# Split weight sums kept in device memory by the first FFN pass, and two variances taken together at a seam

## The chip, the cores and the metric

The kernel runs on one core of one Trainium2 chip. The metric is the device time of one execution in microseconds. A core has TensorE (matrix products into eight banks of PSUM), VectorE and ScalarE (elementwise work; both read PSUM), GpSimd (elementwise work on SBUF alone), and queues from which SyncE, ScalarE and GpSimd issue DMAs. Each engine runs its own instructions in the order in which they stand in its queue, and waits for other engines by semaphores.

## What is computed

One block of a transformer trunk in float32, 2048 tokens wide 1024. The first part (a spatial-gating mixer beside a memory attention, with its output projection and layer norm) is untouched by the change. The second part is this:

```
h = x @ w_in                                   # [2048, 1024] @ [1024, 5632]
y = (silu(h[:, :2816]) * h[:, 2816:]) @ w_down # [2048, 2816] @ [2816, 1024]
x = layer_norm(alpha * x + y) * g + b          # over the 1024 features
```

## The kernel before

Everything is feature-major: partitions hold features, columns hold tokens. TensorE takes float32 in the reduced form float32r, so each operand is **split** (`split`, line 71): ScalarE copies the value into a float32r tile (`hi`, line 73), VectorE subtracts that from the value (`lo`, line 74), and a product takes three matmuls, hi x hi, hi x lo and lo x hi (`PASSES`, line 95).

The FFN part runs in three passes over ranges of tokens (688, 680 and 680; here called pass one, two and three, `no` 0, 1 and 2 in the code). In a pass the width of 2816 is 22 tiles, in five blocks of 5, 4, 4, 4 and 5 (`FBLOCKS`). For each block, `up` makes the gated hidden tiles and `down` adds their part of the output into an accumulator of the pass (`acc`, tiles `fa`).

The up projection of one tile (one of gate and one of value, line 345) uses Strassen's scheme in Winograd's form: the weights of both tiles and both halves of the contraction form a 2 x 2 matrix, the tokens another, and seven products replace eight. Each product is 4 contraction tiles x 3 matmuls of 340 columns (344 in pass one). Its left operands are the weights themselves (a11, a12, a22, products 1, 2, 4) or sums of them (products 5, 6, 7, 3). `halves` (line 97) loads two tiles of 512 KB on SyncE's queue and makes the four sums:

```
engine.tensor_add(s1, a21, a22)        # line 109
engine.tensor_sub(s2, s1, a11)         # line 110
engine.tensor_sub(s3, a11, a21)        # line 112
lambda: engine.tensor_sub(s4, a12, s2) # line 113, called as the products begin
```

`engine` is GpSimd for the first block of each pass and VectorE for the others (line 347). `products` (line 115) then takes the products in the order 1, 6, 2, 5, 7, 3, 4: for each, a buffer `w` of the tag `wsp` (five buffers in all, shared with the weights of `down`), a split into it, twelve matmuls, and the stage behind it (lines 366 to 368), which reads PSUM. Products 1 and 2 share one bank: ScalarE copies it between them (line 366, `m1`); products 5 and 3, and 7 and 4, share banks in the same way, with VectorE's additions between them.

The right operands of a pass (`Pass.load`, line 319) are made while the last block of the pass before is projected down; GpSimd makes one of their sums (line 330). The layer norm of a pass is taken in small steps during the first block of the next pass: `norm_steps` (line 257) is a generator, and behind each product's stage one step is taken (line 373). So there are 5 x 7 = 35 places. GpSimd adds the features into `s_b` (lines 174, 176); `centre` takes the mean from TensorE, subtracts it on VectorE, squares on ScalarE, and adds the squares on GpSimd (line 197); `var` (line 220) brings the variances through TensorE to VectorE, which runs twelve small instructions (lines 227 and 280 to 285) and a diagonal tile `dg` (line 230); `spread` (line 234) has TensorE spread the result over the partitions; `finish` multiplies on VectorE, scales on ScalarE, and stores two feature tiles at a time on SyncE's queue (line 419). A pass has two such norms, one for each half of its tokens. What stays of the steps behind the first block's last product is run at once, and then `residual` loads the accumulator's start (line 383).

The framework orders each engine's instructions ahead of time from the program's order and its own estimate of when each can run; only TensorE's order is fixed as written (`in_order`, line 51).

Of the kernel before, what the change touches and what calls it, by code (L numbers as in the profile page):

```python
# [11 lines left out]
F32 = mybir.dt.float32  # L12
# [14 lines left out]
KD = D // P            # 8 contraction tiles of the model width  # L27
KB = (MIX + HEADS * HD) // P   # 10 contraction tiles of the branch width
NF = DFF // P          # 22 tiles of the FFN width
TC = 512               # tokens in a chunk of the mixer part  # L30
OPERANDS = (25, 3)             # operand tiles of the up projection that find room before and behind the mixer's end
NCHUNK = SEQ // TC
FPASSES = (688, 680, 680)      # tokens in a pass of the FFN part
# [6 lines left out]
def trunk_kernel(ctx, tc, xT, memT, wv, wuq, ws, bs, vg, vb, wmk, wmv, wo,  # L40
# [10 lines left out]
    def in_order(ins):  # L51
        """TensorE runs its instructions in the order in which they are emitted."""
        if last_on_pe:
            tc.add_manual_dep(ins.ins, last_on_pe.pop().name,
                              mybir.DependencyInfo(mybir.DependencyClass.NoSync, mybir.DependencyReason.DATA),
                              reason="order of TensorE")
        last_on_pe.append(ins.ins)
# [13 lines left out]
    def split(hi, lo, src, engine=nc.vector):  # L71
        """src = hi + lo exactly, each with the bits that one pass of TensorE carries."""
        nc.scalar.copy(hi, src)  # L73
        engine.tensor_sub(lo, src, hi.bitcast(F32))  # L74
# [4 lines left out]
    def weights(src, shape, name, loads=1):  # L79
        """src [P, *shape], loaded at once and split; as shape[0] pairs [P, 2, shape[1]], several to a tile."""  # L80
        k, r, pairs = shape[0], raw([P, *shape], f"r_{name}"), []
        for i in range(loads):
            s = slice(i * k // loads, (i + 1) * k // loads)
            nc.sync.dma_start(out=r[:, s], in_=src[:, s])
        parts = -(-k * shape[1] // 512)
        for i in range(parts):
            s = slice(i * k // parts, (i + 1) * k // parts)
            n = s.stop - s.start
            w = wsp([P, 2, n, shape[1]], f"w_{name}_{i}")
            split(w[:, 0], w[:, 1], r[:, s])  # L90
            pairs += [w[:, :, j, :] for j in range(n)]
        return pairs
# [4 lines left out]
    def halves(wa, wb, name, engine, in_place):  # L97
        """Two output tiles' weights, loaded: the left operands of the seven products in Strassen's scheme (in
        Winograd's form), over the two tiles x the halves of the contraction; by product."""
# [15 lines left out]
    def products(left, right, banks, name, stages, order, s4_after):  # L115
        """The seven products, into four banks; `stages` has the sums behind each of them."""
# [4 lines left out]
        for n, p in enumerate(order):  # L121
            if n == s4_after:
                s4()
            to, start, stop = out[p]
            w = wsp([P, 2, 4, P], f"w{p}_{name}")
            split(w[:, 0], w[:, 1], src[p])
            for k in range(4):
                for i, (a, b) in enumerate(PASSES):
                    matmul(to, w[:, a, k, :], right(p, k, b), start=start and k == 0 and i == 0,
                           stop=stop and k == 3 and i == 2, skip_group_check=True)  # L130
            stages[p]()

# [11 lines left out]
    def two_tiles(t, m, t0, n):  # L144
        """Feature tiles m and m + 1 of the tokens t0 to t0 + n."""
        return t[m * P:(m + 2) * P, t0:t0 + n].rearrange("(a p) t -> p a t", p=P)
# [4 lines left out]
    class Norm:  # L151
        """Takes y feature tile by feature tile. Its sums over the tiles run on GpSimd; or, to end soon, on TensorE
        behind a VectorE that takes two tiles at a time (`pairs`)."""
# [24 lines left out]
        def variances(self, sq, start, stop):  # L178
            """One accumulation group for all columns: its start opens the whole bank."""
# [77 lines left out]
    def norm_steps(norms, stores, wait, pad):  # L257
        """The norms in small steps, to be taken between other work."""
# [10 lines left out]
        for _ in range(pad):  # L269
            yield  # L270
        for x, store in zip(norms, stores):
            x.var()
            for _ in range(5):
                yield
            yield from pairs(lambda a, b: x.finish(store, a, b))

    def inv_sqrt(r, v, t):
        """r = v ** -0.5 on VectorE: Newton steps from an estimate made of the bits, half the exponent; t is scratch."""
# [8 lines left out]
    # ================= the mixer part =================  # L287
    open_pools = {}

    def pool(name, bufs, side="left"):  # L290
        """Pools lie one above the other, from either side of the memory."""
# [14 lines left out]
    class Pass:  # L306
        """A range of tokens through the FFN. Its up projection takes Strassen's scheme in Winograd's form, over
        [gate, value] tiles x halves of the model width x halves of the tokens: seven products for eight."""
# [10 lines left out]
        def load(self, k, keep=0):  # L319
            """The seven right operands, for contraction tiles k and k + 4; the last `keep` are left to rest()."""  # L320
# [24 lines left out]
        def up(self, f, work):  # L345
            no, h = self.no, self.h
            sums = nc.gpsimd if f < FBLOCKS[0] else nc.vector    # VectorE has the norm of the pass before at first
# [22 lines left out]
            def then(stage):  # L370
                def run():
# [3 lines left out]

            products(halves(w1[f], w1[NF + f], f"u{name}", sums, False), lambda p, k, b: self.x[p][k][:, b], banks,
                     name, {p: then(stage) for p, stage in stages.items()}, (1, 6, 2, 5, 7, 3, 4), 0)
# [9 lines left out]
        def down(self, blk, gs, f0, cut, done):  # L387
            """The block's part of the FFN's output, for the groups of token ranges of `cut` in turn."""
# [33 lines left out]
    # ================= the mixer part =================  # L422
# [21 lines left out]
    class Chunk:  # L444
        """512 tokens; the methods are emitted in the order in which TensorE is to run them."""
# [15 lines left out]
        def load(self, j):  # L461
            """Feature tiles j and j + 4 of the input."""
# [26 lines left out]
        def v_half(self, hooks):  # L489
            """The v half of the gate, token-major, and its norm."""  # L490
# [38 lines left out]
        def feature_major(self, a, t, name, act):  # L529
            """Output tiles a and a + 1 of the input projection, into t [P, 2, TC]; `act` is run on each part of it."""  # L530
# [19 lines left out]
        def scores(self, b):  # L550
            """Memory attention of 128 tokens: scores and softmax, token-major; heads in the order 0, 2, 1, 3."""
# [23 lines left out]
        def turn(self, b):  # L575
            """The softmax of 128 tokens with the memory on the partitions."""
# [28 lines left out]
        def mixed(self, j):  # L605
            """The v half, mixed over its 128 positions, feature-major."""
# [12 lines left out]
        def u_half(self, j):  # L619
            """The u half, feature-major."""  # L620
# [11 lines left out]
        def project(self, first, after):  # L632
            """Output projection and residual, of feature tiles j and j + 4 in turn."""
# [76 lines left out]
    def make_room(j, m):  # L710
        """Behind output tiles of the last chunk: room for the FFN, and its first operands."""
# [83 lines left out]
    # ================= the FFN part =================  # L795
# [9 lines left out]
    for no in range(len(FPASSES)):  # L805
# [3 lines left out]
        for blk, nb in enumerate(FBLOCKS):  # L809
# [7 lines left out]
            elif no < len(FPASSES) - 1:  # L817
# [10 lines left out]
                work = norm_steps(norms, [pa.store(0, h), pa.store(h, n)], 4, 0)  # L828
# [81 lines left out]
```

## Time and profile before

| what | value |
|---|---|
| timed runs | 2202.6 us median of 3 (2201.05 to 2203.41) |
| profiled execution, span | 2205.3 us, 34595 instructions |
| mean granted TensorE clock | 0.989 of full speed |
| first part, up to the first product of the FFN | 0 to 752 us |
| first block's up projection, pass one / two / three | begins at 752.1 / 1227.0 / 1707.7 us |
| moved by DMA | 221.93 MB, 101 GB/s on the mean |

The span is that of one execution taken by the profiler, which was not one of the timed runs; its span lies 2.7 us above their median. A page of the profile gives busy times of the engines; the trace behind it can be asked for busy times in a stretch of the span, for the waits of one engine (who waited, for which line of which engine, us in all, how often, the longest), for the instructions on one tile (duration least/median/most), and for the instructions in order of time. Lines are those of the kernel before. A matmul's own duration overlaps its neighbours', so the time of one matmul is taken from a stretch divided by the count in it.

### The profile page before, as it was taken

What the parts mean: (1) busy time and instruction counts of PE and PEld (TensorE: products, weight loads), DVE (VectorE), ACT (ScalarE), POOL (GpSimd) and SP (SyncE); (2) the same over time, 40 slices, a digit from 0 to 9 for tenths busy, and PEclk for the clock granted to TensorE, in tenths of its full rate; (3) what the DMA queues carried; (4) which work ended last, traced back from release to release, by engine and by line L of the source; (5) the groups of instructions that cost most, each with busy time, mean ns of one, the idle gap of its engine ahead of it and who ended that gap; (6) DMA issues with size and microseconds to landing.
All of it is one profiled execution on the core that took longest, in us unless ns stands there. A gap on an engine that the chain in (4) does not pass through costs nothing.

```text
span 2205.3 us, 34595 instructions
## 1 busy us (share of the span) xinstructions
PE 2120.0 (96%) x13130; PEld 2009.0 (91%) x13130; DVE 1704.4 (77%) x3014; ACT 970.7 (44%) x1886; POOL 397.3 (18%) x294
## 2 busy tenths in 40 slices
PE   9899999999999999999999889999999899999996
PEld 7888798798788889999999889999998899999996
DVE  7986796797788785776778986676689877677677
ACT  5553653654465452433434453343344534334344
POOL 1412321331322440000001820000004700000003
PEclk9999999999999999999999999999999999999998
DMA  6233324234334443212223242222224242221223
GB/s 211 77 110 123 112 78 158 92 96 149 117 96 133 139 132 92 87 58 86 87 68 91 89 160 88 82 68 82 82 66 119 83 153 67 87 86 58 89 75 99
DMA packets 88965, 221.93 MB, mean 101 GB/s; under 512 B 8416, under 2 KB 18656, under 8 KB 88800
## 3 DMA queue, kind: packets, MB, share of 16 engines
q1 hardware_dynamic: 88320, 218.66, 31.9%
q8 instruction: 103, 1.69, 0.3%
q0 software_dynamic: 480, 1.07, 0.2%
q14 instruction: 62, 0.51, 0.1%
HBM read 202.92 MB, written 16.78 MB: 100 GB/s over the span
## 4 chain that ended last, share of the span: by engine, by line
PE 66%; DVE 19%; DMA 5%; issue 4%; ACT 4%; POOL 2%; ACTq 0%; DVEq 0%; POOLq 0%; SPq 0%
PE h L60 36%; PE d L60 19%; PE v L60 5%; PE u L60 3%; DMA r_x<-in_xT 2%; DVE w L74 2%; DVE x L74 2%; DVE w_o L74 1%; DMA r_f<-x1d 1%; DVE w_u L74 1%; PE y L60 1%; POOL s_a L197 1%; ACT p L569 1%; DVE z L526 1%; DVE w_d L74 1%
## 5 line engine op out<-in xcount | busy, mean ns | idle before, releaser
L60 PE MATMUL h<-x,w 128*128 128x340 f32 (+1 forms) x5544 | 886.5, 322 | 14.7 <-DVE w L74 6.5
L60 PEld LDWEIGHTS h<-x,w 128*128 128x128 f32 x5544 | 875.1, 190 | 22.3 <-DVE w L74 8.9
L60 PE MATMUL d<-g,w_d 128*128 128x340 f32 (+3 forms) x3168 | 504.4, 320 | 7.5 <-DVE w_d L74 6.6
L60 PEld LDWEIGHTS d<-g,w_d 128*128 128x128 f32 x3168 | 497.4, 189 | 11.6 <-DVE w_d L74 8.3
L73 ACT CAST w<-s_u 128x512 fp32r<-128x512 f32 x264 | 163.4, 620 | 227.2 <-PE d L60 106.5
L74 DVE TENSOR_TENSOR w<-s_u,w 128x512 fp32r<-128x512 f32 x264 | 195.2, 741 | 46.1 <-ACT w L73 39.1
L60 PE MATMUL y<-br,w_o 128*128 128x512 f32 x960 | 224.4, 395 | 0.0
L60 PEld LDWEIGHTS y<-br,w_o 128*128 128x128 f32 x960 | 180.5, 188 | 42.0
L73 ACT CAST w<-r_u 128x512 fp32r<-128x512 f32 x198 | 122.3, 618 | 166.6 <-PE h L60 67.7
L60 PE MATMUL v<-w_v,x 128*128 128x512 f32 x768 | 188.4, 402 | 6.7 <-ACT w_v L73 5.0
L74 DVE TENSOR_TENSOR w<-r_u,w 128x512 fp32r<-128x512 f32 x198 | 150.0, 759 | 53.0 <-ACT w L73 49.7
L73 ACT CAST w_d<-r_d 128x512 fp32r<-128x512 f32 (+2 forms) x184 | 95.7, 521 | 206.6 <-PE d L60 151.3
L60 PEld LDWEIGHTS v<-w_v,x 128*128 128x128 f32 x768 | 144.1, 191 | 42.1 <-ACT w_v L73 5.0
L409 DVE TENSOR_TENSOR fa<-fa,d 128x340 f32<-128x340 f32 (+3 forms) x192 | 97.2, 506 | 100.3 <-PE d L60 100.3
L330 POOL TENSOR_TENSOR t<-r_f,r_f 128x340 f32<-128x340 f32 (+1 forms) x12 | 14.9, 1244 | 791.1 <-DMA r_f<-x1d 397.4
L74 DVE TENSOR_TENSOR w_d<-r_d,w_d 128x512 fp32r<-128x512 f32 (+2 forms) x184 | 110.5, 603 | 50.3 <-ACT w_d L73 47.1
L73 ACT CAST g<-c 128x340 fp32r<-128x340 f32 (+1 forms) x132 | 63.1, 478 | 93.9 <-DVE c L354 93.9
L60 PE MATMUL u<-xt,w_u 128*128 128x256 f32 x768 | 95.6, 280 | 0.0
L60 PEld LDWEIGHTS u<-xt,w_u 128*128 128x128 f32 x768 | 92.7, 188 | 0.0
L60 PE MATMUL u<-x,w_u 128*128 128x256 f32 x576 | 78.6, 288 | 11.3 <-DVE u L535 6.9
L60 PEld LDWEIGHTS u<-x,w_u 128*128 128x128 f32 x576 | 72.1, 191 | 13.9 <-issue 6.6
L74 DVE TENSOR_TENSOR w_o<-r_o,w_o 128x512 fp32r<-128x512 f32 (+1 forms) x96 | 67.8, 716 | 21.1 <-ACT w_o L73 20.8
(185 smaller groups left out, 2537.6 us busy)
## 6 DMA issues: line engine op xcount, KB each, us to landing
r_u<-in_w SPq DMA_DIRECT2D x132, 512.0 KB, 3.4
r_d<-in_w SPq DMA_DIRECT2D x72, 256.0 KB, 2.7
r_d<-in_w SPq DMA_DIRECT2D x56, 320.0 KB, 2.9
r_u<-in_wuq SPq DMA_DIRECT2D x32, 512.0 KB, 3.6
r_o<-in_wo SPq DMA_DIRECT2D x32, 512.0 KB, 3.6
r_v<-in_wv SPq DMA_DIRECT2D x31, 512.0 KB, 4.4
y<-in_xT SPq DMA_DIRECT2D x16, 512.0 KB, 5.8
x1d<-y SPq DMA_DIRECT2D x16, 512.0 KB, 4.0
```

Source lines behind the costliest of these rows:

```text
L60: in_order(nc.tensor.matmul(*args, **kw))
L73: nc.scalar.copy(hi, src)
L74: engine.tensor_sub(lo, src, hi.bitcast(F32))
L197: nc.gpsimd.tensor_add(self.s2, self.s2, sq)
L330: nc.gpsimd.tensor_sub(t3, b22, b12)
L409: nc.vector.tensor_add(y, y, p)
L526: nc.vector.tensor_scalar(z[h][:, b], z[h][:, b], mv[:, b, 0:1], rs[:, b:b + 1], ALU.subtract, ALU.mult)
L569: nc.scalar.activation(pr[:, h, :], svs[h // 2][:, h % 2, :], AF.Exp, scale=HD ** -0.5, bias=mxv[:, h:h + 1], accum_out=sm[:, h:h + 1])
```

## The change

In pass one, `products` writes the split operands of the four products whose left operand is a sum (3, 5, 6, 7) to device memory as they are made: 22 tiles x 4 writes of 512 KB, issued on ScalarE's queue (`keep`). In passes two and three `plain` loads only the weights that products 1, 2 and 4 need (one whole tile and half of the other), no sums are made, and for products 3, 5, 6 and 7 the split operand is loaded ready into a buffer of `wsp` from SyncE's queue (`ready`). `weights` takes the same option, which no call uses. In `norm_steps` the variances of all norms at a seam come first, with four steps behind each and four more, and then the finishing steps; before, each norm's variance was followed by five steps and its own finish. The steps ahead of the centring go from 4 to 6 at the two seams between passes. The rest of the diff takes comments and docstrings away.

```diff
+    kept = {}
+
+    def keep(key, w):
+        t = dram.tile(list(w.shape), F32, tag=key, name=f"k_{key}")
+        nc.scalar.dma_start(out=t, in_=w.bitcast(F32))
+        kept[key] = t
+
+    def ready(key, name):
+        src = kept[key]
+        w = wsp(list(src.shape), f"w_{name}")
+        nc.sync.dma_start(out=w.bitcast(F32), in_=src)
+        return w
...
+    def plain(wa, wb, name):
+        ra, rb = (raw([P, KD, P], f"r_{name}_{i}") for i in range(2))
+        nc.sync.dma_start(out=ra, in_=wa)
+        nc.sync.dma_start(out=rb[:, 4:8], in_=wb[:, 4:8])
+        return {1: ra[:, 0:4], 2: ra[:, 4:8], 4: rb[:, 4:8]}, lambda: None
...
-            w = wsp([P, 2, 4, P], f"w{p}_{name}")
-            split(w[:, 0], w[:, 1], src[p])
+            if p in src:
+                w = wsp([P, 2, 4, P], f"w{p}_{name}")
+                split(w[:, 0], w[:, 1], src[p])
+                if key is not None and p in (3, 5, 6, 7) and f"{key}_{p}" not in kept:
+                    keep(f"{key}_{p}", w)
+            else:
+                w = ready(f"{key}_{p}", f"{p}_{name}")
...
+        for x in norms:
+            x.var()
+            for _ in range(4):
+                yield
+        for _ in range(4):
+            yield
         for x, store in zip(norms, stores):
-            x.var()
-            for _ in range(5):
-                yield
             yield from pairs(lambda a, b: x.finish(store, a, b))
...
-            products(halves(w1[f], w1[NF + f], f"u{name}", sums, False), lambda p, k, b: self.x[p][k][:, b], banks,
-                     name, {p: then(stage) for p, stage in stages.items()}, (1, 6, 2, 5, 7, 3, 4), 0)
+            wab = w1[f], w1[NF + f], f"u{name}"
+            left = plain(*wab) if no else halves(*wab, sums, False)
+            products(left, lambda p, k, b: self.x[p][k][:, b], banks,
+                     name, {p: then(stage) for p, stage in stages.items()}, (1, 6, 2, 5, 7, 3, 4), 0, key=f"u{f}")
...
-                work = norm_steps(norms, [pa.store(0, h), pa.store(h, n)], 4, 0)
+                work = norm_steps(norms, [pa.store(0, h), pa.store(h, n)], 6, 0)
```

More of the change, by code (lines that the diff above doesn't have):

```diff
@@ L77, in wsp, with weights @@
         return common.tile(shape, F32R, tag="wsp", bufs=5, name=name)
[L79 to L84, printed above, removed]
-        parts = -(-k * shape[1] // 512)
-        for i in range(parts):
-            s = slice(i * k // parts, (i + 1) * k // parts)
-            n = s.stop - s.start
-            w = wsp([P, 2, n, shape[1]], f"w_{name}_{i}")
-            split(w[:, 0], w[:, 1], r[:, s])
+    kept = {}
[8 more added lines that the diff above has]
+        return w
+    def weights(src, shape, name, loads=1, key=None):
+        k, pairs = shape[0], []
+        parts = -(-k * shape[1] // 512)
+        cuts = [slice(i * k // parts, (i + 1) * k // parts) for i in range(parts)]
+        have = key is not None and f"{key}_0" in kept
+        if not have:
+            r = raw([P, *shape], f"r_{name}")
+            for i in range(loads):
+                s = slice(i * k // loads, (i + 1) * k // loads)
+                nc.sync.dma_start(out=r[:, s], in_=src[:, s])
+        for i, s in enumerate(cuts):
+            n = s.stop - s.start
+            if have:
+                w = ready(f"{key}_{i}", f"{name}_{i}")
+            else:
+                w = wsp([P, 2, n, shape[1]], f"w_{name}_{i}")
+                split(w[:, 0], w[:, 1], r[:, s])
+                if key is not None:
+                    keep(f"{key}_{i}", w)
             pairs += [w[:, :, j, :] for j in range(n)]
@@ L113, in halves, with products @@
         return {1: a11, 2: a12, 3: s4, 4: a22, 5: s1, 6: s2, 7: s3}, lambda: engine.tensor_sub(s4, a12, s2)
-    def products(left, right, banks, name, stages, order, s4_after):
+    def plain(wa, wb, name):
[3 more added lines that the diff above has]
+        return {1: ra[:, 0:4], 2: ra[:, 4:8], 4: rb[:, 4:8]}, lambda: None
+    def products(left, right, banks, name, stages, order, s4_after, key=None):
         q0, q1, q2, q3 = banks
@@ L124, in products @@
             to, start, stop = out[p]
-            w = wsp([P, 2, 4, P], f"w{p}_{name}")
-            split(w[:, 0], w[:, 1], src[p])
+            if p in src:
[3 more added lines that the diff above has]
+                    keep(f"{key}_{p}", w)
+            else:
+                w = ready(f"{key}_{p}", f"{p}_{name}")
             for k in range(4):
```

## The prediction

> **What bounds the kernel now.** First the page, for the share of each engine, then TensorE by stretches, then its waits in the worst of them.
>
> ```profile
> PE 2120.0 (96%) x13130; PEld 2009.0 (91%) x13130; DVE 1704.4 (77%) x3014; ACT 970.7 (44%) x1886; POOL 397.3 (18%) x294
> ```
>
> TensorE is busy 96% of the span. Where it never waits, taking work from another engine gives nothing, so the question is where it waits. The view of busy time by stretches has as its first row an undisturbed block of five FFN tiles (pass two, last block), then the first blocks of passes one, two and three, then the end of the down projection ahead of pass three, and last a stretch of pass one behind its first block.
>
> ```profile
> core 0: us, PE busy (x) PEld busy (x) DVE busy (x) ACT busy (x) POOL busy (x), PEclk, DMA share, GB/s
> 1597.61:1663.04 65.43, 65.43 (x423) 65.43 (x421) 51.08 (x92) 30.62 (x61) 0.87 (x1) 1.00 0.22 67
> 752.07:833.18 81.11, 73.20 (x433) 70.38 (x432) 71.19 (x112) 43.48 (x82) 40.54 (x27) 0.96 0.39 121
> 1227.00:1313.46 86.46, 74.21 (x446) 71.21 (x445) 77.68 (x140) 46.36 (x94) 50.55 (x37) 0.94 0.31 98
> 1707.73:1790.55 82.82, 73.00 (x447) 70.58 (x445) 74.44 (x136) 44.95 (x91) 46.95 (x35) 0.94 0.32 97
> 1694.48:1707.73 13.25, 9.98 (x53) 9.70 (x53) 13.25 (x20) 4.13 (x8) 8.95 (x7) 0.87 0.48 158
> 880.00:913.00 33.00, 33.00 (x212) 32.96 (x211) 27.27 (x51) 15.88 (x32) 0.00 (x0) 1.00 0.19 56
> ```
>
> The clean block does 423 matmuls in 65.43 us, 0.1547 us each, at a granted clock of 1.00. At that pace the 446 matmuls of pass two's first block need 69.0 us and took 86.46: **17.5 us lost**. Pass three's 447 need 69.1 and took 82.82: **13.7 lost**. The 53 ahead of pass three need 8.2 and took 13.25: **5.0 lost**. In pass one's first block (344 columns where the others have 340) 433 need 67.8 and took 81.11: **13.3 lost**. The loss is idle time and a clock that falls after it (0.94). These are also the stretches in which GpSimd works for 40 to 50 us; in the clean block it has 0.87.
>
> What TensorE waited for in pass two's first block, then in pass three's with the end of the down projection:
>
> ```profile
> PE rstd_b L60 <- DVE dg_b L230: 6.0, 1, 6.0
> PE mean_b L60 <- POOL s_b L176: 2.9, 1, 2.9
> PE h L60 <- DVE w L74: 1.6, 2, 1.4
> PE h L60 <- DVE u L367: 1.6, 1, 1.6
> ```
>
> ```profile
> PE rstd_b L60 <- DVE dg_b L230: 6.3, 1, 6.3
> PE d L60 <- DVE w_d L74: 4.4, 2, 3.3
> PE h L60 <- DVE w L74: 1.9, 3, 1.4
> PE h L60 <- DVE u L367: 1.6, 1, 1.6
> ```
>
> Four of the five names are VectorE's. The tile view of the sums, and two neighbours in the timeline, show why it is late.
>
> ```profile
> L74 DVE TENSOR_TENSOR w<-s_u,w x264: 671/692/1785, 752.5 to 2130.3; 128x512 fp32r<-128x512 f32 x132
> L109 DVE TENSOR_TENSOR s_u<-r_u x51: 684/692/695, 855.2 to 2110.1; 128x512 f32<-128x512 f32 x51
> ...
> L110 POOL TENSOR_TENSOR s_u<-s_u,r_u x31: 1272/1434/2162, 72.1 to 1765.0; 128x512 f32<-128x512 f32 x31
> ```
>
> ```profile
> 1700.79 1.41 POOL L110 TENSOR_TENSOR s_u<-s_u,r_u 128x512 f32<-128x512 f32 x1
> 1701.01 1.61 DVE L74 TENSOR_TENSOR w_d<-r_d,w_d 128x384 fp32r<-128x384 f32 x1
> ```
>
> A subtraction of the split takes 0.69 us at the median and up to 1.79; beside GpSimd's sum a smaller one took 1.61, and TensorE's wait of 3.3 us ended with it. In these blocks GpSimd's sums stretch VectorE.
>
> **The change part by part.** *Removed in passes two and three:* per FFN tile four sums and four of seven splits. Outside the first blocks TensorE runs at 1.00 without a wait, so this is worth 0 there. In the two first blocks, GpSimd loses 2 x 5 x 4 sums of 1.3 to 1.4 us, some 27 us in each, about half of its 50.55 and 46.95. VectorE loses 20 subtractions of 0.69 us or more, 14 us of 77.68, and the stretching that those sums cause. ScalarE loses 20 casts.
>
> *Moved:* both variances come ahead of the finishing steps. The chain behind a variance, from its scaling (L227) to the diagonal tile (L230), is the wait of 6 us:
>
> ```profile
> 1262.75 0.14 DVE L227 TENSOR_SCALAR v_b<-var_b 86x4 f32<-86x4 f32 x1
> ...
> 1275.37 0.51 DVE L230 TENSOR_TENSOR dg_b<-ident,r_b 86x344 f32<-86x344 f32 x1
> ```
>
> It took 13.1 us. Today five steps lie between variance and spreading, one step for a product of twelve matmuls (12 x 0.1547 = 1.86 us): 9.3 us. After the change twelve lie there for the first half (4 + 4 + 4), 22.3 us, and for the second too (4 + 4, and the first half's four pairs). Even the stretched chain fits; I cost both rstd waits at nothing. The start waits for six steps in place of four, 3.7 us later, more than the mean's wait of 2.9. The steps end at 6 + 8 + 8 + 4 + 8 = 34 of the block's 35, so nothing is pushed behind the block. What is late next is VectorE beside GpSimd's norm additions, which stay. I leave 2 us in each block: the wait on u (1.6) needs no sum to arise. So 15.5 and 11.7 come back. Of the 5.0 ahead of pass three I take 4, since the wait of 3.3 and the slow clock behind it hang on one stretched subtraction. **Sum gained: 31.2.**
>
> *Added in passes two and three:* four loads of 512 KB for each tile, less 256 KB: 2.75 MB in place of 1.
>
> ```profile
> r_u<-in_w SPq DMA_DIRECT2D x132, 512.0 KB, 3.4
> ```
>
> ```profile
> fa<-x1d SPq DMA_DIRECT2D x4, 688.0 KB, 9.5
> ```
>
> ```profile
> 1312.00:1317.00 5.00, 5.00 (x34) 5.00 (x33) 3.98 (x9) 2.05 (x5) 0.00 (x0) 1.00 1.00 378
> ```
>
> A tile of the FFN takes 13.1 us (65.43 / 5): 2.88 million bytes in that are 220 GB/s, of 378 moved at a full share. A load can be issued when the buffer of the product five back is free, so it has four products, 7.4 us; a lone load of this size landed in 3.4. With one transfer of 1.4 us ahead (512 KB at 378 GB/s) it is 4.8. Hidden: cost 0. Without that cover it is the slower rival below. On SP's queue the loads stand in line with the norm's stores, which move three to six steps later and wait for ScalarE:
>
> ```profile
> SPq L419 <- ACT fa L253: 7.9, 6, 3.6
> ```
>
> The longest wait in that block, 3.6 us, is within the 4.0 (7.4 - 3.4) to spare.
>
> *Added in pass one:* 88 writes of 512 KB on ScalarE's queue, each behind VectorE's subtraction. Writes from ScalarE are nowhere in this trace, so I bound them by neighbours: a write of that size, and SP's time to issue one DMA.
>
> ```profile
> x1d<-y SPq DMA_DIRECT2D x16, 512.0 KB, 4.0
> ```
>
> ```profile
> 1348.15 0.33 SPq L102 DMA_DIRECT2D r_u<-in_w  x1
> ```
>
> Landing holds the split's buffer for 4.0 us, and TensorE holds it for more than that, so it costs nothing. ScalarE stands for a subtraction and an issue, 0.69 + 0.33 = 1.0 us, four times a tile. Queued behind it are the casts of the next products and the copy of the first product (L366). TensorE adds the third product of the order into the bank that this copy reads, one product of 1.86 us after it is filled. Behind the first block ScalarE is busy 15.88 of 33 us, so 6.8 of 13.1 us a tile are free for 4.1: cost 0, and 88 us if none of it were covered. In pass one's first block VectorE is already late, and a held ScalarE holds the casts it needs: between 0 and 20 x 1.0 = 20 us, below 0 for no reason that I see. The row nearest is that block's own waits, where ScalarE is named for little:
>
> ```profile
> PE h L60 <- ACT m L367: 1.0, 1, 1.0
> PE h L60 <- ACT w L73: 0.7, 1, 0.7
> ```
>
> I take 4, some twice their sum. The moved steps of its one norm cost nothing: no wait on rstd stands in that block's rows, and 26 steps fit in 35.
>
> Total: 31.2 - 4 = 27 off. Against the profiled span of 2205.3 that is 2178; the median of the timed runs is 2202.6, 2.7 less than this span, and I carry the same difference: **2175.5 us**.
>
> **The rivals.** *ScalarE's queue in pass one.* SP's queue shows what an issue behind a wait does, here waiting for VectorE to free a buffer:
>
> ```profile
> SPq L102 <- DVE w L74: 530.1, 69, 13.8
> ```
>
> If each of the 20 writes in the first block shows its whole 1.0 us, 16 us more are lost: 2192. For it: VectorE was the wait there. Against it: ScalarE is busy only 43.48 of those 81.11 us. The Trainium skill, in "DMA: Bandwidth & Descriptors" (Anatomy of one DMA), says that DMA engines never wait on semaphores; the issuing sequencer does, before dispatch. By that rule ScalarE is held in full for each write, and the row above agrees with it; taken alone and without cover it would make all 88 us visible, 2260, and the free time above is what speaks against that. Chance 0.14.
>
> *The first blocks don't clear.* It is GpSimd's norm additions, not its sums, that stretch VectorE; then the change takes work away without doing what it says for the waits, and half of 31.2 comes back: 2191. For it: those additions stay. Against it: the sums are about half of GpSimd's time there, and the 3.3 us wait ended beside a sum. Chance 0.10.
>
> *Gains and costs cancel*, within 0.2% of 2202.6 (4.4 us, about what a measurement of this kernel can tell from no change). Chance 0.06.
>
> *Slower: loads land too late.* Five buffers go round; in five products (9.3 us) a load must be issued, land, and be used for 1.86 us. It decides at a landing of 7.4 us. At the 9.5 us of the largest row, a round takes 11.4: 2.1 us more on each of 44 x 7 / 5 = 62 rounds, 130 us: 2305. At 8.4 it is 62 us: 2237. For it: loads now hang on TensorE's buffers instead of VectorE's early splits. Against it: 3.4 us. Chance 0.10.
>
> **How the numbers follow.** The forecast has 0.60; its own range is 2166 (all 36.2 us back, no cost) to 2185. Faster takes forecast and the first two rivals: 0.84. Same 0.06, slower 0.10. The range for 8 in 10 reaches from 2166 over both milder rivals to 2196; above it lie the cancelled and the slower case, 0.16.
>
> **What would show it.** In the changed profile: the first blocks of passes two and three at about 71 us with a clock near 1.00 and no wait on rstd or mean; GpSimd there with norm additions alone; no wait of TensorE on a load of a kept tile; pass one's first block near 85 us. Wrong would be waits of TensorE for those loads, a row of ScalarE's queue that waits on the subtraction with TensorE's waits beside it, or rstd waits that remain.

## The result, and the profile after

| | before | after |
|---|---|---|
| timed runs, median of 4 | 2202.45 us (2201.05 to 2203.41) | 2177.65 us (2175.97 to 2181.36) |
| ratio of after to before, 95% interval | | 0.9892 (0.9878 to 0.9906) |
| profiled execution, span | 2205.3 us | 2174.2 us |
| mean granted TensorE clock | 0.989 | 0.993 |

The changed kernel is 1.1% faster, 24.8 us between the medians. The profiled execution of after was the fastest of its timed runs, and that of before took longer than any of its own (2205.3 us against 2203.41 at most). So the spans lie 31.1 us apart, 6.3 more than the medians. Sums over stretches are compared with 31.1; in which stretches the 6.3 lie is not shown.

The share of each engine and the bytes moved, from the page of after:

```profile
PE 2111.3 (97%) x13130; PEld 2003.1 (92%) x13130; DVE 1484.8 (68%) x2702; ACT 874.4 (40%) x1710; POOL 329.0 (15%) x254
...
HBM read 283.66 MB, written 62.91 MB: 159 GB/s over the span
```

TensorE does the same 13130 matmuls; VectorE has 312 instructions less. The stretches of after, from the view of busy time by stretches, are pass one's first block, the down projection behind it up to the next block, the first blocks of passes two and three, and the end of the down projection ahead of pass three:

```profile
core 0: us, PE busy (x) PEld busy (x) DVE busy (x) ACT busy (x) POOL busy (x), PEclk, DMA share, GB/s
750.45:833.05 82.60, 72.63 (x433) 68.86 (x432) 71.23 (x108) 41.27 (x78) 38.21 (x26) 0.98 0.65 233
833.05:874.88 41.83, 39.80 (x243) 39.28 (x241) 21.98 (x43) 9.95 (x21) 0.00 (x0) 0.96 0.35 123
1231.54:1300.74 69.20, 69.20 (x446) 68.20 (x445) 50.33 (x117) 35.02 (x72) 17.24 (x18) 1.00 0.70 235
1690.47:1759.55 69.08, 69.08 (x446) 68.19 (x445) 50.14 (x117) 34.96 (x72) 17.10 (x18) 1.00 0.69 235
1680.86:1690.47 9.61, 8.50 (x52) 8.22 (x53) 9.32 (x18) 2.89 (x6) 4.65 (x4) 1.00 0.64 209
```

In the two seam blocks TensorE's busy time equals the stretch: no gap is left, and the clock is full. They went from 86.46 to 69.20 and from 82.82 to 69.08, the end of the down projection from 13.25 to 9.61. That is 17.3 + 13.7 + 3.6 = **34.6 us gained** between these two executions. Pass one lost. Its block and the down projection behind it took 81.11 + 37.72 = 118.83 before:

```profile
833.18:870.90 37.72, 37.72 (x242) 37.72 (x241) 20.59 (x40) 8.80 (x18) 0.00 (x0) 1.00 0.32 93
```

They now take 82.60 + 41.83 = 124.43, **5.6 us more**. 34.6 - 5.6 = 29.0; the FFN also began 1.6 us earlier (750.45 against 752.07), ahead of anything changed, so 0.5 of the 31.1 lies elsewhere.

TensorE's waits in that part of pass one (after; who waited for which line, us in all, times, longest). Behind the change the stages of the products stand at L405 (copy of the first product), L406 and L407, the write of a kept operand at L83, its load at L90, and the split still at L73 and L74:

```profile
PE h L60 <- ACT m L405: 3.3, 3, 1.5
PE h L60 <- DVE u L406: 3.1, 3, 1.9
PE h L60 <- ACT w L73: 1.9, 1, 1.9
PE d L60 <- ACT g L73: 1.9, 1, 1.9
PE h L60 <- DVE w L74: 1.1, 1, 1.1
```

Three of the names are ScalarE's, which the change gave the writes; a sixth wait, of 0.4 us, is VectorE's. ScalarE's timeline at the first such wait (start, duration, in brackets the idle time before and what ended it), and then TensorE's:

```profile
753.85 0.33 ACTq L83 DMA_DIRECT2D k_u<-w  x1
754.22 1.24 ACT L73 CAST x<-t 128x344 fp32r<-128x344 f32 x3 [2.30 <-DVE w L74]
755.36 0.44 ACT L405 COPY m<-h 128x344 f32<-128x344 f32 x1
```

```profile
755.85 4.34 PE L60 MATMUL h<-x,w 128*128 128x344 f32 x26 [1.46 <-ACT m L405]
```

ScalarE stood 2.30 us for VectorE's subtraction because the write in its queue needs it, with the copy of the first product behind; TensorE waited 1.46 us for that copy. A second hold comes at the end of the block, where the pass's residual tiles are loaded. First two rows of the DMA view of 815 to 840 us (KB each, median us from issue to landing), then ScalarE's waits for landings there:

```profile
fa<-x1d SPq DMA_DIRECT2D x4, 688.0 KB, 11.3
k_u<-w ACTq DMA_DIRECT2D x5, 512.0 KB, 8.2
```

```profile
ACT w_d L73 <- DMA k_u<-w: 5.5, 3, 2.4
...
ACT w L73 <- DMA k_u<-w: 1.4, 1, 1.4
```

The five buffers serve the down projection too, and a buffer is free only when its write has landed. Over all 88 writes the median is 2.9 us, and ScalarE waited for a landing five times only. Here, at 8.2, its casts stand, the steps that make the gated tile are queued behind them, and the down projection waits 1.9 us for that tile. In TensorE's timeline the wait has a slow stretch behind it, 38 matmuls in 8.18 us where 5.9 are due; the granted clock was 0.50 from 839 to 841 us:

```profile
837.01 8.18 PE L60 MATMUL d<-g,w_d 128*128 128x344 f32 x38 [1.90 <-ACT g L73]
```

The kept operands' loads never hold TensorE: no row of its waits names them.

### The profile page after: what moved, and what is told of

It is laid out like the page before. It is cut to its first block, busy times and chain, and to the rows that moved or that the text cites. A ratio compares the mean times of both kernels' runs of the same rounds, so it can differ in the third digit from the quotient of the medians.

```text
span 2174.2 us, 34544 instructions
## 1 busy us (share of the span) xinstructions
PE 2111.3 (97%) x13130; PEld 2003.1 (92%) x13130; DVE 1484.8 (68%) x2702; ACT 874.4 (40%) x1710; POOL 329.0 (15%) x254
## 4 chain that ended last, share of the span: by engine, by line
PE 70%; DVE 17%; DMA 5%; issue 4%; ACT 3%; POOL 2%; ACTq 0%; DVEq 0%; SPq 0%; POOLq 0%
PE h L60 37%; PE d L60 19%; PE v L60 5%; PE u L60 3%; PE y L60 2%; DMA r_x<-in_xT 2%; DVE x L74 2%; DVE w_o L74 1%; DMA r_f<-x1d 1%; DVE w_u L74 1%; DVE z L567 1%; POOL s_a L233 1%; ACT p L610 1%; DVE w L74 1%; DVE w_d L74 1%
## 5 line engine op out<-in xcount | busy, mean ns | idle before, releaser
L73 ACT CAST w<-r_u 128x512 fp32r<-128x512 f32 x198 | 121.6, 619 | 260.1 <-PE h L60 163.0
L74 DVE TENSOR_TENSOR w<-r_u,w 128x512 fp32r<-128x512 f32 x198 | 141.1, 715 | 66.4 <-ACT w L73 56.6
L73 ACT CAST w_d<-r_d 128x512 fp32r<-128x512 f32 (+2 forms) x184 | 95.4, 521 | 202.5 <-PE d L60 145.8
L74 DVE TENSOR_TENSOR w_d<-r_d,w_d 128x512 fp32r<-128x512 f32 (+2 forms) x184 | 108.8, 597 | 48.4 <-ACT w_d L73 45.7
L369 POOL TENSOR_TENSOR t<-r_f,r_f 128x340 f32<-128x340 f32 (+1 forms) x12 | 13.9, 1161 | 813.0 <-DMA r_f<-x1d 406.4
L73 ACT CAST g<-c 128x340 fp32r<-128x340 f32 (+1 forms) x132 | 63.1, 478 | 109.7 <-DVE c L393 109.6
L405 DVE TENSOR_TENSOR u<-h,m 128x340 f32<-128x340 f32 (+1 forms) x66 | 33.8, 512 | 76.7 <-PE h L60 76.5
L74 DVE TENSOR_TENSOR w_o<-r_o,w_o 128x512 fp32r<-128x512 f32 (+1 forms) x96 | 69.6, 733 | 22.3 <-ACT w_o L73 22.2
L73 ACT CAST w<-s_u 128x512 fp32r<-128x512 f32 x88 | 53.0, 621 | 75.2 <-PE d L60 34.5
```

Source lines behind the costliest of these rows:

```text
L369: nc.gpsimd.tensor_sub(t3, b22, b12)
L405: stages = {1: lambda: nc.scalar.copy(m1, q0), 6: lambda: nc.vector.tensor_add(u2, q1, m1), 2: lambda: nc.scalar.activation(m1, q0, AF.Sil ...
```

## The experiments

The times in the second column are medians, with the ratio to runs of before on the same chip and its 95% interval. "Pass one" is the block with the down projection behind it (118.83 before, 124.43 after). The stage times are of one profiled execution each. The framework orders the queues anew for each kernel (it is called the planner here), so two kernels can differ in more places than the edited lines.

| kernel | us | ratio | pass one | pass two's block | pass three's block |
|---|---|---|---|---|---|
| before | 2202.45 | | 118.83 | 86.46 | 82.82 |
| after | 2177.65 | 0.9892 (0.9878 to 0.9906) | 124.43 | 69.20 | 69.08 |
| steps_only | 2198.99 | 0.9972 (0.9963 to 0.9982) | 118.33 | 82.14 | 78.81 |
| kept_only | 2181.61 | 0.9896 (0.9882 to 0.9911) | 124.90 | 69.45 | 69.30 |
| gpsimd_busy | 2206.36, one run | before 2205.29 | 126.6 | 81.56 | 78.68 |
| no_writes | 2171.23 | 0.9849 (0.9834 to 0.9864) | 117.00 | 69.20 | 69.11 |
| vector_sums_before | 2204.28 | 0.9992 (0.9983 to 1.0002) | 116.44 | 88.18 | 84.40 |
| vector_sums | 2175.20 | 0.9864 (0.9849 to 0.9880) | 122.83 | 69.37 | 69.07 |
| late_residual | 2179.42 | 0.9885 (0.9865 to 0.9904) | 128.88 | 69.18 | 69.13 |
| sp_writes | 2174.42 | 0.9855 (0.9834 to 0.9877) | 120.71 | 69.21 | 69.07 |
| combo | 2167.42 | 0.9834 (0.9820 to 0.9847) | 113.91 | 69.19 | 69.09 |
| gpsimd_other | 2192.17 | 0.9947 (0.9929 to 0.9965) | 124.87 | 78.16 | 76.94 |
| four_buffers | 2201.37 | 0.9996 (0.9986 to 1.0006) | 128.32 | 71.29 | 71.33 |
| traffic | 2247.72 | 1.0199 (1.0181 to 1.0218) | | | |

### Which half carries the gain

The kernel before with the moved variances alone:

```diff
-        for x, store in zip(norms, stores):
+        for x in norms:
             x.var()
-            for _ in range(5):
+            for _ in range(4):
                 yield
+        for _ in range(4):
+            yield
+        for x, store in zip(norms, stores):
             yield from pairs(lambda a, b: x.finish(store, a, b))
...
-                work = norm_steps(norms, [pa.store(0, h), pa.store(h, n)], 4, 0)
+                work = norm_steps(norms, [pa.store(0, h), pa.store(h, n)], 6, 0)
```

> The kernel before with the moved norm steps alone (variances together, six steps ahead): sums and splits stay as they were. Theory (the chain of 13 us behind a variance is hidden by twelve steps, and the late mean by two more): the waits on rstd (6.0 and 6.3 us) and on the mean (2.9) go, with the slow clock behind each (about 2 us each); VectorE stays stretched by GpSimd's sums, so the first blocks of passes two and three keep some 6 to 9 us of loss: 76 to 79 us each in place of 86.5 and 82.8, time 2185 to 2192. Rival (VectorE is late all through the block, so a wait that is taken away returns as another): blocks of 82 us or more, time within 5 us of 2202.

Measured: 0.9972; the two blocks get 4.3 and 4.0 us shorter, less than expected in pass two's. TensorE's four largest waits in pass two's block of this kernel (its stages are L369 to L371), and the block's row:

```profile
PE h L60 <- DVE u L370: 2.7, 2, 1.6
PE h L60 <- DVE t_b L287: 2.7, 1, 2.7
PE h L60 <- DVE w L74: 2.0, 2, 1.2
PE h L60 <- ACT m L369: 1.6, 1, 1.6
```

```profile
1225.81:1307.95 82.14, 72.63 (x446) 69.70 (x445) 77.86 (x140) 44.80 (x92) 49.29 (x37) 0.98 0.26 82
```

The waits on rstd (6.0) and on the mean (2.9) are gone as named, but the others come to 9.5 us, 0.5 on L371 included, where they were 3.2 (1.6 each on L74 and L367). VectorE is still busy 77.86 us (77.68 before), and most of what it doesn't do in time merely has another name.

The changed kernel with the old order of the variances:

```diff
-        for x in norms:
+        for x, store in zip(norms, stores):
             x.var()
-            for _ in range(4):
+            for _ in range(5):
                 yield
-        for _ in range(4):
-            yield
-        for x, store in zip(norms, stores):
             yield from pairs(lambda a, b: x.finish(store, a, b))
```

with the start waiting for four steps again.

> The changed kernel with the norm steps of before (variance, five steps, finish; four steps ahead). Theory (GpSimd's sums stretch VectorE): without them the chain behind a variance takes 7 to 10 us, about the five steps of 9.3, and the mean's additions are done in time: first blocks of passes two and three 69 to 72 us, waits on rstd of 1 us at most, time 2177 to 2182. Rival (the moved steps do it): rstd waits of 3 us or more remain and a mean wait, blocks of 74 us or more, time 2188 or more.

Measured: 0.9896, the same as after and as the theory had it; the blocks take 69.45 and 69.30, a quarter of a microsecond more each. Pass two's block:

```profile
1234.12:1303.57 69.45, 69.35 (x446) 68.28 (x445) 52.18 (x117) 35.52 (x73) 17.82 (x18) 1.00 0.75 256
```

With 52.18 us of VectorE in place of 77.68, the old order has no rstd wait either. The kept operands by themselves bring practically all of the gain; the moved steps add a quarter of a microsecond a block to it.

### Why the seam blocks clear: contention or load

Is it GpSimd's sums stretching VectorE, or simply what VectorE has to do? First the sums are put back on GpSimd in the two blocks, with the full load of raw weights, and nobody reads them:

```diff
+        nc.gpsimd.tensor_add(s1, a21, a22)
+        nc.gpsimd.tensor_sub(s2, s1, a11)
+        nc.gpsimd.tensor_sub(s3, a11, a21)
+        return {1: a11, 2: a12, 4: a22}, lambda: nc.gpsimd.tensor_sub(s4, a12, s2)
```

> The changed kernel, in which GpSimd also makes the four sums in the first blocks of passes two and three, and nobody reads them. Theory (contention): VectorE's instructions on SBUF there are stretched again to 1.2 us and more, and the blocks take 72 to 78 us in place of 69.1. Rival (what helped is that VectorE and ScalarE have fewer splits to do): blocks stay at 69 to 70 us although GpSimd is busy for some 45 us in them.

Measured: blocks of 81.56 and 78.68, longer than the theory's 72 to 78. Pass two's block by its row, and two of TensorE's waits in it:

```profile
1234.37:1315.93 81.56, 72.54 (x446) 70.90 (x445) 58.86 (x119) 34.81 (x72) 44.23 (x37) 0.96 0.62 211
```

```profile
PE h L60 <- ACT m L413: 6.0, 2, 3.2
PE h L60 <- DMA w<-k_u: 3.0, 1, 3.0
```

VectorE is busy 8.5 us longer than in after (58.86 against 50.33) with two instructions more: contention stretches it. But the waits name ScalarE and a late load, and SyncE stood for raw tiles that the slow sums held. So this kernel changes more than contention, and isn't the test that it was meant to be.

The other way round, the kernel before with the sums on VectorE, so that GpSimd has only the norm's additions:

```diff
-            sums = nc.gpsimd if f < FBLOCKS[0] else nc.vector
+            sums = nc.vector
```

> The kernel before with the four sums of every tile on VectorE, in the first blocks too; no memory is used. Theory (GpSimd's sums cost more by stretching VectorE and by holding buffers than the sums themselves would cost VectorE): VectorE gets 20 sums of 0.69 us more a block and loses the stretch; it is then some 70 us busy in a block of 69, so a little is lost: 71 to 76 us for the first blocks of passes two and three (86.5 and 82.8 before), 71 to 76 for pass one's (81.1), time 2172 to 2183. Rival (VectorE's own work is the bound, and only taking splits and sums away helps): blocks of 79 us or more, time 2193 or more.

Measured: 0.9992, no change, which is what the rival said. Pass two's block by its row, and TensorE's waits in it:

```profile
1224.44:1312.62 88.18, 77.53 (x447) 73.59 (x446) 78.83 (x159) 46.04 (x94) 20.83 (x18) 0.92 0.30 97
```

```profile
PE h L60 <- DVE w L74: 7.6, 6, 3.8
PE h L60 <- DVE u L367: 3.0, 1, 3.0
```

GpSimd fell from 50.55 to 20.83 us, and a subtraction of a raw weight's split from 947 to 728 ns in the mean. The sums that came over, four of 0.87 to 1.02 us a tile, put it all back: VectorE is busy 78.83 us, and the block is no shorter. In these blocks moving the sums doesn't help; they have to go. (Pass one's block with the down projection behind it did get shorter, 116.44 against 118.83.)

Last, contention with nothing hanging on it: after, with three additions on GpSimd behind each of the two gated parts of a tile in the two blocks; they hold no buffer that anyone wants.

```diff
+                if no and f < FBLOCKS[0]:
+                    for _ in range(3):
+                        t = open_pools["sums"].tile([P, 4, P], F32, tag="sums", name=f"idle{i}_{_}_{name}")
+                        nc.gpsimd.tensor_add(t.rearrange("p a b -> p (a b)")[:, 0:h],
+                                             g[:, 0, i * h:(i + 1) * h].bitcast(F32), g[:, 1, i * h:(i + 1) * h].bitcast(F32))
```

> The changed kernel, in which GpSimd also does 30 additions of 340 columns in the first blocks of passes two and three on gated tiles that are kept anyway, so that no buffer is held for it and nothing waits for the results. Theory, as it stands after the sums on VectorE changed nothing before (stretching and VectorE's own work are two ways to the same full VectorE): VectorE, 50 us busy of 69, takes the stretch in its free time: blocks of 69 to 71 us. Rival (contention alone delays TensorE): 73 us or more.

Measured: 78.16 and 76.94, the rival's side. That is 9.0 and 7.9 us lost, though VectorE is busy for only 56.29 of 78.16. In pass two's block TensorE waits 4.4 us for VectorE, and behind the waits the clock falls (0.93 over the block), so that the 446 matmuls are busy for 73.73 us in place of 69.2. How the waits come about, in the timeline of this kernel (L398 is the additions, L322 to L324 small steps of the norm's root, L410 and L411 the stages of products 1 and 2):

```profile
1267.55 5.31 POOL L398 TENSOR_TENSOR idle<-g 128x340 f32<-128x340 f32 x6
1267.65 0.84 DVE L322 SCALAR_TENSOR_TENSOR t_b<-r_b 86x4 f32<-86x4 f32 x1
1268.53 0.84 DVE L323 TENSOR_TENSOR t_b<-t_b,v_b 86x4 f32<-86x4 f32 x1
...
1272.04 0.84 DVE L324 SCALAR_TENSOR_TENSOR r_b<-t_b,r_b 86x4 f32<-86x4 f32 x1
...
1272.81 0.50 DVE L410 TENSOR_TENSOR u<-h,m 128x340 f32<-128x340 f32 x1
1273.23 0.15 DVE L322 SCALAR_TENSOR_TENSOR t_b<-r_b 86x4 f32<-86x4 f32 x1
...
1275.31 0.50 DVE L411 TENSOR_TENSOR u<-h,u 128x340 f32<-128x340 f32 x1
...
1275.87 6.48 PE L60 MATMUL h<-x,w 128*128 128x340 f32 x22 [2.47 <-DVE u L411]
```

Six steps that take 0.15 us alone take 0.84 each while GpSimd adds, 0.88 us apart, which is the pace of its six additions (5.31 / 6 = 0.885): each VectorE step lasts as long as one addition. L410 and L411 stand behind them, and TensorE waits 2.47 us. The Trainium skill, in "SBUF — State Buffer" (Who interferes with whom), calls the port pair that VectorE and GpSimd share an exclusive lock. This trace agrees: each step, with two operands in SBUF, gets through only once per addition, and the operations that read PSUM keep their 0.50 us.

So either cause is enough by itself: a full VectorE without the sums' contention (vector_sums_before, where only the norm's additions contend), and contention with a free VectorE (gpsimd_other). The change takes both away. How much of before's 17.5 us was the one and how much the other stays open: these additions come six in a row, those sums came one or two at a time.

### What pass one's writes cost, and why

After without the writes but for a single one that every kept load reads:

```diff
-        src = kept[key]
+        src = next(iter(kept.values()))
...
-                if key is not None and p in (3, 5, 6, 7) and f"{key}_{p}" not in kept:
+                if key is not None and p == 6 and not kept:
```

> The changed kernel with a single write in place of 88; every ready load of passes two and three takes that one tile, so the products 3, 5, 6 and 7 there have wrong weights. Theory (the writes cost pass one 5.6 us: 1.5 in its first block, 4.1 at the start of the down projection behind it): first block 81 us, that stretch 37.7, time 2171 to 2174. Rival (the order of the instructions changed and the writes are innocent): 82.6 and 41.8 stay, time 2177 to 2179.

Measured: 0.9849, pass one 117.00. By the profiles the writes cost 124.43 - 117.00 = 7.4 us; by the ratios 0.0043 of 2205, 9.5 us, between runs on two chips. Both are above the 4 predicted. (Before and steps_only, which write nothing either, took 118.83 and 118.33 there, so such a difference is good to a microsecond or two.) The rows of the block and of the down projection behind it:

```profile
752.67:831.95 79.28, 71.98 (x433) 68.85 (x432) 72.20 (x112) 42.83 (x81) 39.74 (x27) 0.98 0.38 123
831.95:869.67 37.72, 37.72 (x242) 37.72 (x241) 20.58 (x40) 8.82 (x18) 0.00 (x0) 1.00 0.34 111
```

The writes issued by SyncE, so that ScalarE waits for no subtraction:

```diff
-        nc.scalar.dma_start(out=t, in_=w.bitcast(F32))
+        nc.sync.dma_start(out=t, in_=w.bitcast(F32))
```

> The changed kernel with the 88 writes issued on SyncE's queue. Theory as predicted (ScalarE, held for each write, delays pass one's first block): that block with the stretch behind it falls from 124.4 us to 117 to 120, time 2170 to 2174. Rival (it is the landing that holds buffers, or SyncE's loads now stand behind the writes): 123 us or more, time 2176 or more.

Measured: 0.9855, pass one 120.71, half of the 7.4 us back, between the theory and the rival. The two rows are the block and the down projection behind it:

```profile
752.72:835.71 82.99, 73.38 (x434) 70.28 (x432) 73.31 (x111) 43.23 (x81) 40.78 (x27) 0.96 0.63 221
835.71:873.43 37.72, 37.72 (x243) 37.72 (x241) 21.19 (x42) 8.87 (x18) 0.00 (x0) 1.00 0.45 163
```

All that came back lies in the down projection; the block takes as long as in after (82.60). TensorE's largest waits in it are now VectorE's, as they were before the change; no wait on L405 is left, and the block gains nothing by it:

```profile
PE h L60 <- DVE c L407: 3.7, 2, 2.9
PE h L60 <- DVE w L74: 3.2, 2, 2.3
PE h L60 <- DVE u L406: 1.7, 3, 0.8
```

After with the sums of pass one's first block on VectorE:

```diff
-            sums = nc.gpsimd if f < FBLOCKS[0] else nc.vector
+            sums = nc.vector
```

> The changed kernel with pass one's first block's sums on VectorE (passes two and three make none). Theory: pass one's first block and the down projection behind it, 124.4 us together in the changed kernel and 118.8 before, fall to 110 to 117; time 2164 to 2172. Rival (ScalarE, held by the writes, is the bound there): 122 us or more, time within 3 us of 2177.6.

Measured: 0.9864, pass one 122.83, as the rival had it. A little is gained, and the waits on ScalarE's L405 (3.5 us) stay.

To test the landing, the residual's four loads were to go into the down projection, each just ahead of the part that needs it:

```diff
-                pa.residual()
+                pa.residual(0, 2)
+                pa.down(blk, gs, f0, whole,
+                        lambda ci, m: pa.residual(m + 2, m + 4) if m % 2 == 0 and m < KD - 2 else None)
```

> The changed kernel, with the accumulator's start loaded pair by pair between the steps of the first down projection in place of four loads at once. Theory (the writes of the block's last tile land late beside four loads of 688 KB, 8.2 us in place of 2.9, and hold the buffers that the next casts need): no wait of ScalarE on the writes in that place, the down projection's stretch 37.7 to 39 us in place of 41.8, time 2173 to 2176. Rival (the late landing is the writes' own doing): 41 us or more, time within 2 us of 2177.6.

Measured: 0.9885, as after. The planner that orders the queues moved the loads forward again: they are issued from 825 to 831 us, ahead of a down projection that begins at 840.88, and land after 11.8 us with writes beside them at 8.1. The edit didn't make the difference that it was to test, so it says nothing of the landing. What it does serve for is as a second after, on the chip of sp_writes and vector_sums: 2179.42 against 2174.42 and 2175.20. It also shows how much pass one varies with the same writes in it: 128.88 in its profiled run, which was its slowest. In kept_only (124.90) the loss is in another place than in after: the block takes 87.17 and the down projection 37.73, without a wait.

Both edits together:

```diff
-        nc.scalar.dma_start(out=t, in_=w.bitcast(F32))
+        nc.sync.dma_start(out=t, in_=w.bitcast(F32))
...
-            sums = nc.gpsimd if f < FBLOCKS[0] else nc.vector
+            sums = nc.vector
```

> The changed kernel with both: the 88 writes on SyncE's queue, and pass one's first block's sums on VectorE. Alone the first made pass one's first block with the stretch behind it 120.7 us and the second 122.8, where the changed kernel takes 124.4 and one without the writes 117.0. Theory (two separate costs): 117 to 120 us there, time 2170 to 2174. Rival (one cause seen twice): 121 us or more, time 2174 to 2177.

Measured: **2167.42 us**, 0.9834, faster than both kernels. Its block and the down projection behind it:

```profile
750.24:826.44 76.20, 70.03 (x433) 67.59 (x432) 70.39 (x129) 40.93 (x78) 11.72 (x9) 1.00 0.68 240
826.44:864.15 37.71, 37.71 (x243) 37.71 (x241) 20.86 (x41) 8.85 (x18) 0.00 (x0) 1.00 0.46 163
```

113.91 us is less than the theory's 117 to 120, less than no_writes took with its sums on GpSimd (117.00), and 10.5 less than after, where the single edits gave 3.7 and 1.6. That the two help each other is not shown by this: by the medians, each against before on its chip, after is 24.8 us faster, sp_writes 30.9, vector_sums 30.1 and combo 35.8, so the edits bring 6.1 and 5.3 alone and 11.0 together, about their sum. With ScalarE free and GpSimd out of the way no wait in this block passes 2.0 us, and the clock stays at 1.00. Casts still stood 5.0 us for landings here (8.8 in sp_writes, whose last four writes landed in 7.2 us at the median), and no wait of TensorE in this stretch is for ScalarE: a landing by itself need not hurt. How after's cost divides between the issue and the landing isn't settled, since the block varies by microseconds from run to run.

### How near the loads are to being late

One buffer less, four in place of five, shortens the loads' cover:

```diff
-        return common.tile(shape, F32R, tag="wsp", bufs=5, name=name)
+        return common.tile(shape, F32R, tag="wsp", bufs=4, name=name)
```

> The changed kernel with four buffers for split operands in place of five, so that a load has three products, 5.6 us, where it had 7.4; loads land in 4.0 us (median), 6.3 at most. Theory (a load hurts only when it lands later than its buffers allow): waits of TensorE on those loads of under 10 us in all, time 2178 to 2195, part of it lost in pass one and the first part, whose splits have a buffer less too. Rival (the loads have little to spare): waits of more than 30 us on them, time over 2210.

Measured: 0.9996, which gives away the whole gain (more than expected), but not where the loads are. Two of TensorE's waits over the span:

```profile
PE u L60 <- DVE w_u L74: 14.3, 4, 4.7
...
PE h L60 <- DMA w<-k_u: 2.1, 4, 0.9
```

The loads are waited for 2.1 us in all. Of the 21.4 us between the spans, most lie where operands are still split and lack the buffer: pass one begins 5.5 us later than in after, takes 3.9 more up to the end of its first down projection and 3.4 more behind that. The seam blocks lose 2.1 and 2.3.

Twice the traffic: with each load of a kept operand goes a copy of it to another place in device memory, which nothing reads.

```diff
+        extra.append(dram.tile(list(src.shape), F32, tag=f"e{len(extra)}", name=f"e{len(extra)}"))
+        nc.scalar.dma_start(out=extra[-1], in_=src)
```

> The changed kernel with, beside each of the 176 loads, a copy of the same 512 KB from device memory to device memory on ScalarE's queue: in passes two and three the DMA engines' share goes from 0.6 to nearly 1. Theory (the slower rival of the prediction, whose point is a landing of 7.4 us): if loads land in 5 to 7 us the time stays within 10 us of 2177; if they land in 8 to 10, TensorE waits on them at nearly every one and the time is 2230 or more. Expected: 7 to 9 us and 2200 to 2260. Rival (landing does not grow with traffic): 4 us and no change.

Measured: 2247.72, 1.0199, as expected. The landings of the kept loads over the span and (with their KB and median) from 875 to 1480 us, TensorE's wait on them from 870 us on, and two stretches:

```profile
DMA to landing us min/median/max: 3.0/4.1/17.7
```

```profile
w<-k_u SPq DMA_DIRECT2D x37, 512.0 KB, 7.8
```

```profile
PE h L60 <- DMA w<-k_u: 29.5, 13, 7.7
```

```profile
1250.00:1480.00 230.00, 193.23 (x1152) 187.80 (x1151) 104.34 (x223) 62.98 (x127) 18.06 (x18) 0.93 0.89 331
1480.00:2245.00 765.00, 746.36 (x4761) 740.20 (x4759) 415.13 (x810) 235.56 (x469) 51.92 (x48) 0.99 0.52 173
```

The planner issued most copies early, so the DMA engines are nearly full (0.89) only up to some 1480 us. There the loads land in 7.8 us at the median, just above the 7.4 at which the prediction had them late, and all 29.5 us of waits on them lie there; behind it, at a share of 0.52, there is none. Of the 71 us between this span and that of after, 20 are lost ahead of pass two, where nothing is loaded ready, and practically all the rest up to 1480: 1152 matmuls that need 178.2 us at 0.1547 take 230. The slower rival is thus a real mechanism; it showed at a share of 0.89. In after's seam blocks the share is 0.70.

## Why the prediction was right, step by step

- **What bounded the kernel: right.** TensorE's waits in the seam blocks and just ahead of pass three were the whole gain. The splits and sums removed in the other blocks were worth nothing: the stretch from pass two's first block to the end ahead of pass three took 381.0 us before and 380.1 after.
- **Sum gained, 31.2: too small by 3.4.** I left 2 us in each block for the waits on u; nothing is left of them (69.20 and 69.08 where 446 matmuls need 69.0). That is +1.8 and +2.0. The end ahead of pass three gave 3.6 of the 4 taken. These are sizes from one execution each. My reserve was for GpSimd's norm additions, which stayed (17.24 us in the block) and hold up nobody once VectorE has 19 us free.
- **Both rstd waits and the mean's wait go because the steps are moved: right as far as it goes, but not needed.** steps_only loses them as reckoned, and the other waits grow from 3.2 to 9.5 us. kept_only lacks them with the old order. Moving the steps brings 4 us a block alone and 0.25 beside the kept operands.
- **"GpSimd's sums stretch VectorE": one of two causes.** Stretching by GpSimd's additions is enough to hold TensorE (gpsimd_other), but taking it away and leaving the work with VectorE gives nothing (vector_sums_before). The sum counted both as going, so the forecast held.
- **Writes behind pass one's first block cost 0: right.** Behind it TensorE's waits up to pass two come to 2.7 us, none of them for ScalarE or for a write.
- **Writes in the first block cost 4: too small.** It is 5.6 by stage against before, 7.4 against no_writes and 9.5 by ratios. I forecast the block near 85; it took 82.60, and 4.1 us of the loss (41.83 - 37.72) show in the down projection behind it, which I had not looked at. The step that doesn't hold is "landing holds the split's buffer for 4.0 us" and so "costs nothing": beside the residual's loads a landing takes 8.2, and ScalarE's casts wait for it. Whether the landing by itself is the cause stays open, since sp_writes has landings of 7.2 us and no loss in the down projection (37.72). One of the signs that I had named for being wrong is there: ScalarE stands 2.30 us for the subtraction, and TensorE 1.46 us beside it.
- **Loads hidden: right.** They landed in 4.0 us at the median, within the 3.4 to 4.8 that I reckoned with, and in 6.3 at most, within the cover of 7.4 (least, median, most):

```profile
DMA to landing us min/median/max: 3.0/4.0/6.3
```

- **Stores of the norm in SyncE's queue: right.** Their longest wait for ScalarE in pass two's block is 2.4 us, of 4.0 to spare. (The 3.6 before is that of pass three's block; pass two's had 3.7.)
- **The sum.** By stages 34.6 were gained and 5.6 lost against 31.2 and 4: the two errors partly cancel, and 29.0 is 2 more than the 27 forecast. By the medians it is 24.8, and 2177.65 is 2.2 above the forecast of 2175.5. I had put the median 2.7 us below the span; for after it lies 3.5 above it. So the sizes of single terms are no surer than some microseconds, and that the median came so near is in part luck.
- **The rivals.** ScalarE's queue in pass one is real but small: with the landings the writes cost 6 to 10 us, where that rival had 20 (16 on top of the 4), and sp_writes shows that part of it can be had back. "The first blocks don't clear" is wrong: they clear with the norm additions in place. "Gains and costs cancel" is wrong: the interval of the ratio ends at 0.9906. Loads that land too late cost TensorE much only with DMA engines at 0.89 (29.5 us in traffic, 2.1 in four_buffers).

## What to carry to other kernels

Where TensorE waits for an engine with a full queue, look at how much that engine has to do in the stretch before reordering it: reordering gave most of the waits other names, and taking work away ended them. A DMA issued from a compute engine behind another engine's result makes that engine wait for the result, so issue it where nothing urgent stands behind it, and count its landing where the DMA engines are full, not at its median. Before calling two fixes worth more together than apart, compare medians: one profiled execution of each said 10.5 us against 3.7 and 1.6 here, the medians 11.0 against 6.1 and 5.3.

## What the runs showed of the hardware beside that

- Small VectorE operations on two operands in SBUF take as long as a GpSimd addition that runs beside them: 0.84 us in place of 0.15 for 86x4 elements, beside additions of 0.885 us, while the additions that read a PSUM bank stay at 0.50.
- The 88 writes of 512 KB from ScalarE's queue landed in 2.9 us at the median and 9.1 at most; the kept operands' loads of that size took 4.0 at the median, and SyncE's writes of it (x1d) 4.0 too.
- A wait of TensorE can cost more than itself. After the one of 1.90 us the granted clock was 0.50 from 839 to 841 us, and the matmuls were slower by 2.3 us in all (8.18 less 5.9). After one of 1.87 us in combo (at 782.2 us) it stayed at 1.00. What decides between the two is not shown.
